# Gate and up products in two matmuls instead of three, with halves that are added behind, and a first column group in one piece

## The chip, the cores and the metric

The program runs on one core of a Trainium2 chip. The metric is device time in microseconds, from launch to end. The kernel before was timed three times: 1051.45, 1048.04 and 1046.29, median 1048.04. One further execution was profiled, and the profile's lines come from that one.

## The reference

A decoder trunk of two layers over 256 rows of 1024 columns, in float32. Each layer is a SwiGLU block, a token mixer (gated DeltaNet in layer 0, sliding-window attention in layer 1) and a second SwiGLU block, each behind an RMSNorm; a last RMSNorm follows. Cut to what matters here:

```python
D_FF = 2816                                   # ((8 * 1024 // 3 + 127) // 128) * 128

def swiglu(h, w_gu, w_down):                  # h: (1, 256, 1024), w_gu: (1024, 2 * 2816), w_down: (2816, 1024)
    gate, up = jnp.split(h @ w_gu, 2, axis=-1)
    return (jax.nn.silu(gate) * up) @ w_down

for layer in range(2):
    x = x + 0.5 * swiglu(rmsnorm(x, ffn1_norm[layer]), ffn1_w_gu[layer], ffn1_w_down[layer])
    x = x + mixer(rmsnorm(x, mix_norm[layer]))
    x = x + 0.5 * swiglu(rmsnorm(x, ffn2_norm[layer]), ffn2_w_gu[layer], ffn2_w_down[layer])
return rmsnorm(x, final_norm)
```

So four SwiGLU blocks run, with a gate and up product of 1024 by 5632 weights each.

## The kernel before

**Precision.** TensorE works on one-pass operands (type float32r). Each float32 operand is therefore split exactly into a high and a low part, and one product is made of three: high by high, high by low and low by high (`mm3`, lines 307 to 311). The rows' operand after a norm is `hh` and `hl`, transposed, 128 partitions by 8 tiles of the 1024 columns by 256 rows. Weights come from memory in pieces of 512 KB into `raw`, are cast to the high part `whi` by ScalarE (ACT, line 275), and VectorE (DVE) subtracts that from `raw` to get `wlo` (line 276). `raw` has 4 buffers, `whi` and `wlo` 5 each, so a piece can be cast only when the matmuls have let go of the one five before it. The loads are issued by SyncE (SP) in the order of use.

**Gate and up.** `ffn` (line 329) walks over 11 groups `c` of 256 gate columns and 256 up columns. A group's weights are two pieces for gate and two for up (`wcols`). In groups 1 to 10 the weight is the stationary operand and the 256 rows stream past it: `proj_T` makes, for each of 2 column tiles `f` and 8 tiles `k` of the inner dimension, the three matmuls of `mm3`, 256 columns wide, all into the same half bank of PSUM (`pg` or `pu`, from a pool of 4 banks). ScalarE takes Silu of `pg` into `sg` (line 338), VectorE multiplies it with `pu` into `act` (line 340), GpSimd (POOL) rounds that to `ah` (line 389) and VectorE subtracts to get `al` (line 390): the two parts of the operand for the down product. The matmuls of one `k`, `f` and of gate or up are called a **unit** below: three matmuls, three weight loads. There are 4 blocks x 10 groups x 2 x 2 x 8 = 1280 units.

Group 0 is done the other way round (`part_N`): the rows are stationary, 128 at a time (`t` is 0 or 1), the weight streams, 256 columns of gate into `pg` and 256 of up into `pu`; the result `act` is turned by two transposes (`pat`, line 378). This lets rows 0 to 127 start while rows 128 to 255 are still in the norm: the transposes `psT` (line 89) of those rows stand between the two halves of group 0.

**The first block** starts before its norm is known: it multiplies x times the norm's weight (`hh0`, `hl0`) and scales behind; GpSimd then scales the operand `f` itself in four pieces (line 183), and from those come `hh`, `hl` for groups 1 to 10 (lines 185, 186). The second half of x is loaded by `late()`, called between gate's and up's weights of group 0.

**Down** streams the weight rows, 512 columns wide, past `ah` and `al`, in units of three matmuls too (`acc`); in the last block some of them are 256 wide. The mixers use `proj_T` and `proj_N` with their three matmuls.

Instructions of an engine run in the order that a list scheduler gave them from its own estimate of times when the program was built; an engine does not overtake within its order.

Of the kernel before, what the change touches and what calls it, by code (L numbers as in the profile page):

```python
# [15 lines left out]
P = 128  # L16
D = 1024
T = 256
# [36 lines left out]

class Norm:
    """RMSNorm of the residual into a transposed, exactly split operand hh + hl."""

    def __init__(self, kern, wrow):
        self.k = kern  # L60
        self.w = kern.n4([P, D], "nw")
        kern.nc.scalar.dma_start(out=self.w, in_=wrow.partition_broadcast(P))
        self.hh = self.hl = None
# [17 lines left out]
    def tile(self, t):  # L81
        k, nc = self.k, self.k.nc
        if self.hh is None:
            self.hh = k.big([P, KT, T], "hh", F32R)
            self.hl = k.big([P, KT, T], "hl", F32R)
        for q, (xn, s) in enumerate(self.rows(t)):
# [11 lines left out]
    def piece(self, t, s, sq):  # L98
        """Of a row's piece, x * w and the sum of the squares."""
# [25 lines left out]
class First(Norm):  # L125
    """The first norm: the rows' factor comes late, so the first products take x * w and are scaled behind."""

    def __init__(self, kern, wrow):
# [4 lines left out]
        self.hh0, self.hl0 = k.big([P, KT, T], "hh0", F32R), k.big([P, KT, T], "hl0", F32R)  # L133
        self.hh, self.hl = k.big([P, KT, T], "hh", F32R), k.big([P, KT, T], "hl", F32R)
# [3 lines left out]
    def raw(self, t):  # L138
# [7 lines left out]
        for q in range(2):  # L146
# [7 lines left out]
            oh = self.hh0[:, ks, ts]  # L154
            nc.scalar.copy(oh, f)
            nc.vector.tensor_sub(self.hl0[:, ks, ts], f, oh.bitcast(F32))
# [14 lines left out]
    def scale(self):  # L171
# [8 lines left out]
        for q in range(4):  # L180
# [3 lines left out]
            oh = self.hh[:, ks]  # L184
            nc.scalar.copy(oh, f)
            nc.vector.tensor_sub(self.hl[:, ks], f, oh.bitcast(F32))  # L186


class Kern:
# [60 lines left out]
    def warm(self, n):  # L250
        """Products that nobody reads, while the first loads are under way: the array's clock rises with its use."""
# [10 lines left out]
    def split(self, src, hi, lo, shape, eng=None):  # L262
# [49 lines left out]

    def proj_T(self, out, w, f, nrm):
        fs = slice(f * P, (f + 1) * P)
        for k in range(KT):
            wh, wl = w(k, fs)
            self.mm3(out, wh, wl, nrm.hh[:, k, :], nrm.hl[:, k, :], k == 0, k == KT - 1)

    def proj_N(self, out, w, t, nrm):
        self.part_N(out, w, t, nrm.hh, nrm.hl, range(KT))  # L320

    def part_N(self, out, w, t, hh, hl, ks):
        ts = slice(t * P, (t + 1) * P)
        for k in ks:
            wh, wl = w(k, slice(0, 256))
            self.mm3(out, hh[:, k, ts], hl[:, k, ts], wh, wl, k == 0, k == KT - 1)

# [1 line left out]
    def ffn(self, nrm, w_gu, w_down, after, mid=None, late=None, final=None):  # L329
# [6 lines left out]
        def glu(pg, pu):  # L336
            sg = self.c1([P, T], "sg")
            ahead[0] = nc.scalar.activation(sg, pg[:, :T], AF.Silu)
            a = self.c1([P, T], "act")
            ahead[1] = nc.vector.tensor_mul(a, sg, pu[:, :T])  # L340
            return a

        for c in range(DFF // 256):
# [5 lines left out]
            wg = self.wcols(w_gu, c * 256)  # L349
            if c == 0 and late is not None:  # L350
                late()
            wu = self.wcols(w_gu, DFF + c * 256)
            pgs = [None] * 2
            if c == 0 and late is not None:
                pgs = [(self.psA("pg"), self.psA("pu")) for t in range(NT)]
                for n, w in ((0, wg), (1, wu)):
                    for ks in (range(0, 4), range(4, 8)):
# [921 lines left out]
```

## Time and profile before

| | us |
|---|---|
| median of three runs | 1048.04 (1046.29 to 1051.45) |
| profiled execution: span from first to last instruction | 1048.2 |
| PE (TensorE's matmuls) busy in it | 1021.5 |
| DVE busy | 625.9 |
| ACT busy | 498.8 |
| POOL busy | 220.4 |

The profiled execution's own time is its span: nothing outside the first and last instruction is recorded, and the span lies 0.2 us from the median. Its stages, by the starts of PE's rows: gate and up of the first block from 11 to 144 us, down to 205, DeltaNet to 387, second block to 576, third to 766, attention to 852, fourth block to 1042.

How to read the lines: a matmul's row gives its start, its length and the width of what streams (`128x256` is 256 columns). Matmuls are pipelined, so rows overlap; what one costs in a dense stream is the distance from its start to the next start, not its length. PEld is the weight load, which has a row of its own. In groups of instructions the columns are line, engine, operation, out<-in, shapes, count, then busy us and mean ns of one, then the idle time of the engine just before and what ended it.

### The profile page before, as it was taken

How to read it: one execution, taken by the hardware profiler on the slowest of the kernel's cores; microseconds unless marked ns; L12 is line 12 of the kernel's file. 1: busy time of each engine (PE TensorE's matmuls, PEld its weight loads, DVE VectorE, ACT ScalarE, POOL GpSimd, SP SyncE). 2: the span in 40 equal slices, each digit the busy share in tenths (PEclk: the TensorE clock that was granted, in tenths of full speed). 3: DMA queues.
4: the chain of work that ended last, by engine and by line, in shares of the span. 5: the costliest groups of instructions: out<-in, count | busy, mean ns of one | idle time of the engine just before them, and what ended most of it. 6: DMA issues, size and time to landing. Idle time of an engine off the chain costs nothing.

```text
span 1048.2 us, 18944 instructions
## 1 busy us (share of the span) xinstructions
PE 1021.5 (97%) x7683; PEld 956.2 (91%) x7683; DVE 625.9 (60%) x887; ACT 498.8 (48%) x847; POOL 220.4 (21%) x197
## 2 busy tenths in 40 slices
PE   8999999999979999999999999999999999999997
PEld 7999998899979889999988999998899689999986
DVE  5755554666895665565545655554568856555544
ACT  5544443557755544443434433444456644344432
POOL 3123410006743201122100022120021401221100
PEclk9999999999989999999999999999999999999999
DMA  7666666654442335566565566567653426655661
GB/s 225 188 192 186 183 213 190 186 156 130 133 141 83 120 101 162 161 187 200 195 195 179 173 190 190 163 195 217 215 180 123 133 89 191 201 172 173 212 196 43
DMA packets 135003, 177.20 MB, mean 169 GB/s; under 512 B 6930, under 2 KB 119940, under 8 KB 134916
## 3 DMA queue, kind: packets, MB, share of 16 engines
q1 hardware_dynamic: 131712, 171.46, 52.6%
q10 hardware_dynamic: 3204, 4.53, 1.4%
q8 instruction: 60, 0.98, 0.4%
q14 instruction: 27, 0.22, 0.1%
HBM read 174.92 MB, written 1.05 MB: 168 GB/s over the span
## 4 chain that ended last, share of the span: by engine, by line
PE 62%; issue 1%; DVE 1%; ACT 0%; POOLq 0%; POOL 0%; ACTq 0%
PE acc L311 7%; PE acc L309 7%; PE acc L310 7%; PE pg L309 6%; PE pg L311 6%; PE pu L311 6%; PE pu L309 6%; PE pu L310 6%; PE pg L310 6%; PE pq L309 1%; PE pq L311 1%; PE pq L310 1%; PE psc L1103 1%; PE po L1147 1%; PE psT L89 1%
## 5 line engine op out<-in xcount | busy, mean ns | idle before, releaser
L275 ACT CAST whi<-raw 128x1024 fp32r<-128x1024 f32 x316 | 330.0, 1051 | 313.9 <-PE pg L310 161.5
L276 DVE TENSOR_TENSOR wlo<-raw,whi 128x1024 fp32r<-128x1024 f32 x302 | 382.1, 1268 | 154.3 <-ACT whi L275 153.8
L389 POOL TENSOR_SCALAR ah<-act 128x256 fp32r<-128x256 f32 x80 | 103.5, 1294 | 389.9 <-DVE act L340 389.9
L310 PE MATMUL pg<-hl,whi 128*128 128x256 f32 x640 | 181.2, 283 | 1.0 <-DVE hl L186 1.0
L310 PE MATMUL pu<-hl,whi 128*128 128x256 f32 x640 | 181.3, 283 | 0.0
L311 PE MATMUL pg<-hh,wlo 128*128 128x256 f32 x640 | 181.2, 283 | 0.0
L309 PE MATMUL pu<-hh,whi 128*128 128x256 f32 x640 | 181.2, 283 | 0.0
L311 PE MATMUL pu<-hh,wlo 128*128 128x256 f32 x640 | 181.2, 283 | 0.0
L309 PE MATMUL pg<-hh,whi 128*128 128x256 f32 x640 | 181.1, 283 | 0.0
L310 PE MATMUL acc<-wlo,ah 128*128 128x512 f32 (+1 forms) x340 | 128.4, 378 | 0.0
L311 PE MATMUL acc<-whi,al 128*128 128x512 f32 (+1 forms) x340 | 128.2, 377 | 0.0
L309 PE MATMUL acc<-whi,ah 128*128 128x512 f32 (+1 forms) x340 | 127.9, 378 | 0.0
L310 PEld LDWEIGHTS pg<-hl,whi 128*128 128x128 f32 x640 | 122.9, 192 | 1.2 <-DVE hl L186 1.2
L311 PEld LDWEIGHTS pg<-hh,wlo 128*128 128x128 f32 x640 | 122.9, 192 | 0.0
L309 PEld LDWEIGHTS pg<-hh,whi 128*128 128x128 f32 x640 | 122.9, 192 | 0.0
L311 PEld LDWEIGHTS pu<-hh,wlo 128*128 128x128 f32 x640 | 122.8, 192 | 0.0
L309 PEld LDWEIGHTS pu<-hh,whi 128*128 128x128 f32 x640 | 122.8, 192 | 0.0
L310 PEld LDWEIGHTS pu<-hl,whi 128*128 128x128 f32 x640 | 122.8, 192 | 0.0
L340 DVE TENSOR_TENSOR act<-sg,pu 128x256 f32<-128x256 f32 x86 | 35.9, 418 | 98.0 <-PE pu L311 96.2
L309 PEld LDWEIGHTS acc<-whi,ah 128*128 128x128 f32 x340 | 64.0, 188 | 11.9
L311 PEld LDWEIGHTS acc<-whi,al 128*128 128x128 f32 x340 | 63.9, 188 | 12.0
L310 PEld LDWEIGHTS acc<-wlo,ah 128*128 128x128 f32 x340 | 64.0, 188 | 11.7
(343 smaller groups left out, 1623.5 us busy)
## 6 DMA issues: line engine op xcount, KB each, us to landing
raw<-in_ffn_w_gu_dram SPq DMA_DIRECT2D x176, 512.0 KB, 4.9
raw<-in_ffn_w_down_dram SPq DMA_DIRECT2D x88, 512.0 KB, 4.3
raw<-in_a_w_in_dram SPq DMA_DIRECT2D x32, 512.0 KB, 4.5
raw<-in_b_w_in_dram SPq DMA_DIRECT2D x12, 512.0 KB, 4.9
raw<-in_a_w_out_dram SPq DMA_DIRECT2D x8, 512.0 KB, 3.9
raw<-in_b_w_out_dram SPq DMA_DIRECT2D x8, 512.0 KB, 3.8
nw<-in_ffn_norm_dram ACTq DMA_DIRECT2D x3, 512.0 KB, 4.1
x<-in_x_dram SPq DMA_DIRECT2D x2, 512.0 KB, 7.1
```

Of the source, the lines that this page charges most:

```text
L89: last = nc.tensor.transpose(ps[:, i * P:(i + 1) * P], xn[:, s.start + i * P:s.start + (i + 1) * P], k.ident)
L275: nc.scalar.copy(hi, raw)
L276: (eng or nc.vector).tensor_tensor(out=lo, in0=raw, in1=hi.bitcast(F32), op=ALU.subtract)
L309: nc.tensor.matmul(out, lhsT=lh, rhs=rh, start=start, stop=False)
L310: nc.tensor.matmul(out, lhsT=lh, rhs=rl, start=False, stop=False)
L311: return nc.tensor.matmul(out, lhsT=ll, rhs=rh, start=False, stop=stop)
L340: ahead[1] = nc.vector.tensor_mul(a, sg, pu[:, :T])
L389: ahead[2] = nc.gpsimd.tensor_scalar(oh, a, 1.0, None, op0=ALU.mult)
L1103: nc.tensor.matmul(out, lhsT=qT[:, j, b * P:(b + 1) * P], rhs=kz[:, kv, :, kt * P:(kt + 1) * P], start=True, stop=True)
L1147: lastpo[0] = nc.tensor.matmul(po[64 * i:64 * i + 64, b * P:(b + 1) * P], lhsT=v[:, kt, kv * HD:(kv + 1) * HD], rhs=pT[:, b + kt, i, :], s ...
```

## The change

Three things change.

1. The two parts of the rows' operand lie side by side: class `Split` holds two tiles of 128 x 4 x 2 x 256, so that high part and low part of one `k` are 512 neighbouring columns (`both`). A unit of groups 1 to 10 becomes two matmuls (`mm2`, `proj_T2`): the weight's high part against all 512 columns, into a whole PSUM bank, and the weight's low part against the high rows, 256 columns, added to the bank's first half.
2. The two halves of the bank are added behind: ScalarE copies the second half to SBUF (`gate` or `act`), VectorE adds the first half. Silu is then taken in place, and the product of gate and up moves from VectorE to GpSimd. Gate's two column tiles now come before up's two.
3. Group 0 loads gate and up columns together (`wpairs`): four pieces of 2 tiles `k` by 512 columns, each loaded by two DMAs. Its three matmuls of `part_N` are 512 wide and fill one bank `pgu`. `late()` is called behind all four pieces instead of behind the first two. Silu and the product behind it both wait for the same bank.

The mixers keep `mm3`, with the parts taken from `Split`.

```diff
+class Split:
+    def __init__(self, kern):
+        self.parts = [kern.big([P, 4, 2, T], "hs", F32R) for _ in range(2)]
+    def four(self, q, ts):
+        return tuple(self.parts[q][:, :, e, ts] for e in range(2))
+    def both(self, k):
+        return self.parts[k // 4][:, k % 4].rearrange("p e t -> p (e t)")
+    def hi(self, k, ts=slice(0, T)):
+        return self.parts[k // 4][:, k % 4, 0, ts]
+    def lo(self, k, ts=slice(0, T)):
+        return self.parts[k // 4][:, k % 4, 1, ts]
...
-            oh = self.hh[:, 4 * q:4 * q + 4, t * P:(t + 1) * P]
+            oh, ol = self.h.four(q, slice(t * P, (t + 1) * P))
             hi = nc.scalar.copy(oh, pv)
-            lo = nc.vector.tensor_sub(self.hl[:, 4 * q:4 * q + 4, t * P:(t + 1) * P], pv, oh.bitcast(F32))
+            lo = nc.vector.tensor_sub(ol, pv, oh.bitcast(F32))
...
-        nc.sync.dma_start(out=raw, in_=src)
+        if inner is None:
+            nc.sync.dma_start(out=raw, in_=src)
+        else:
+            for k in range(shape[1]):
+                nc.sync.dma_start(out=raw[:, k].rearrange("p (g f) -> p g f", g=2), in_=src[:, k])
...
+    def wpairs(self, w, c0):
+        src = w.rearrange("(k p) (g f) -> p k g f", p=P, g=2)[:, :, :, c0:c0 + 256]
+        pieces = []
+        for i in range(4):
+            hi = self.wp.tile([P, 2, 512], F32R, tag="whi", name="whi")
+            lo = self.wp.tile([P, 2, 512], F32R, tag="wlo", name="wlo")
+            self.split(src[:, 2 * i:2 * i + 2], hi, lo, [P, 2, 512], inner="p k (g f) -> p k g f")
+            pieces.append((hi, lo))
+        return lambda k, cs: tuple(a[:, k % 2, cs] for a in pieces[k // 2])
...
+    def mm2(self, out, lh, ll, r2, rh, start, stop):
+        nc = self.nc
+        nc.tensor.matmul(out, lhsT=lh, rhs=r2, start=start, stop=False)
+        return nc.tensor.matmul(out[:, :T], lhsT=ll, rhs=rh, start=False, stop=stop)
+    def proj_T2(self, out, w, f, h):
+        fs = slice(f * P, (f + 1) * P)
+        for k in range(KT):
+            wh, wl = w(k, fs)
+            mm = self.mm2(out, wh, wl, h.both(k), h.hi(k), k == 0, k == KT - 1)
+        return mm
...
+            if c == 0:
+                w = self.wpairs(w_gu, 0)
+                ps = [self.psA("pgu") for t in range(NT)]
+                if late is not None:
+                    late()
+                    for ks in (range(0, 2), range(2, 4), range(4, 6), range(6, 8)):
                         for t in range(NT):
-                            self.part_N(pgs[t][n][:, :T], w, t, nrm.hh0, nrm.hl0, ks)
+                            self.part_N(ps[t], w, t, nrm.h0, ks)
...
+                    if late is None:
+                        nc.scalar.activation(sg, ps[t][:, :T], AF.Silu)
+                        nc.vector.tensor_mul(a, sg, ps[t][:, T:])
...
-                    self.proj_T(pg[:, :T], wg, f, nrm)
-                    self.proj_T(pu[:, :T], wu, f, nrm)
-                    a = glu(pg, pu)
-                    ff = 2 * c + f
-                    oh = ah[ff // 8][:, ff % 8, :]
-                    ahead[2] = nc.gpsimd.tensor_scalar(oh, a, 1.0, None, op0=ALU.mult)
-                    nc.vector.tensor_sub(al[ff // 8][:, ff % 8, :], a, oh.bitcast(F32))
+            gates = []
+            wg = self.wcols(w_gu, c * 256)
+            for f in range(2):
+                pg = self.psA("pg")
+                self.proj_T2(pg, wg, f, nrm.h)
+                g = self.c1([P, T], "gate")
+                nc.scalar.copy(g, pg[:, T:])
+                nc.vector.tensor_tensor(out=g, in0=g, in1=pg[:, :T], op=ALU.add)
+                ahead[0] = nc.scalar.activation(g, g, AF.Silu)
+                gates.append(g)
+            wu = self.wcols(w_gu, DFF + c * 256)
+            for f in range(2):
+                pu = self.psA("pu")
+                self.proj_T2(pu, wu, f, nrm.h)
+                a = self.c1([P, T], "act")
+                nc.scalar.copy(a, pu[:, T:])
+                ahead[1] = nc.vector.tensor_tensor(out=a, in0=a, in1=pu[:, :T], op=ALU.add)
+                nc.gpsimd.tensor_tensor(out=a, in0=a, in1=gates[f], op=ALU.mult)
+                ff = 2 * c + f
+                oh = ah[ff // 8][:, ff % 8, :]
+                ahead[2] = nc.gpsimd.tensor_scalar(oh, a, 1.0, None, op0=ALU.mult)
+                nc.vector.tensor_sub(al[ff // 8][:, ff % 8, :], a, oh.bitcast(F32))
```

Where the instructions stand now is shown at three places. Names are the program's tiles, with the number of the buffer's use; `xN` is a row that stands N times.

**PE, group 0 of the second block, at the seam between rows 0 to 127 and rows 128 to 255.** Before, the last up products of the first rows, then the transposes of the second rows, then those of `act`, then gate and up of the second rows in turn, with their high rows first:

```order
L310 MATMUL pu_4494<-wlo_4488,hh_4359 128x256
L311 MATMUL pu_4494<-whi_4487,hl_4360 128x256
L89 MATMUL psT_4446<-ident_70,xn_4438 128x128 x4
L89 MATMUL psT_4454<-ident_70,xn_4438 128x128 x4
L378 MATMUL pat_4547<-ident_70,act_4545 128x128 x2
L309 MATMUL pg_4552<-whi_4469,hh_4359 128x256
L310 MATMUL pg_4552<-wlo_4470,hh_4359 128x256
L309 MATMUL pu_4553<-whi_4481,hh_4359 128x256
```

After, at the same place:

```order
L342 MATMUL pgu_4211<-wlo_4205,hs_4074 128x512
L343 MATMUL pgu_4211<-whi_4204,hs_4074 128x512
L107 MATMUL psT_4160<-ident_70,xn_4152 128x128 x4
L107 MATMUL psT_4168<-ident_70,xn_4152 128x128 x4
L412 MATMUL pat_4241<-ident_70,act_4238 128x128 x2
L341 MATMUL pgu_4212<-whi_4183,hs_4073 128x512
L342 MATMUL pgu_4212<-wlo_4184,hs_4073 128x512
L343 MATMUL pgu_4212<-whi_4183,hs_4073 128x512
```

The transposes `pat` stand at the same distance from the last product as before, but that product now ends gate as well as up, so Silu is no longer done ahead of it.

**ACT in a middle group of the first block.** Before, between two casts of weights stands one Silu:

```order
L338 ACTIVATE sg_540<-pg_490 128x256
L275 CAST whi_608<-raw_610 128x1024
L275 CAST whi_614<-raw_616 128x1024
L338 ACTIVATE sg_596<-pg_546 128x256
L275 CAST whi_620<-raw_622 128x1024
```

After:

```order
L424 COPY gate_446<-pg_429 128x256
L433 COPY act_479<-pu_462 128x256
L426 ACTIVATE gate_446<-gate_446 128x256
L296 CAST whi_568<-raw_570 128x1024
L296 CAST whi_620<-raw_622 128x1024
L433 COPY act_502<-pu_485 128x256
```

Two copies, one of gate and one of up, and a Silu now stand between two pairs of casts; the Silu waits for VectorE's add.

**SP at the start.** Before, the second load of x stands behind two pieces of weights:

```order
L1211 DMA x_81<-in_x_dram 128x1024
L265 DMA raw_136<-in_ffn1_w_gu_dram 128x4x256
L265 DMA raw_142<-in_ffn1_w_gu_dram 128x4x256
L1211 DMA x_81<-in_x_dram 128x1024
L265 DMA raw_165<-in_ffn1_w_gu_dram 128x4x256
L265 DMA raw_171<-in_ffn1_w_gu_dram 128x4x256
```

After, behind four, each loaded by two DMAs:

```order
L1260 DMA x_81<-in_x_dram 128x1024
L286 DMA raw_136<-in_ffn1_w_gu_dram 128x2x256 x2
L286 DMA raw_143<-in_ffn1_w_gu_dram 128x2x256 x2
L286 DMA raw_150<-in_ffn1_w_gu_dram 128x2x256 x2
L286 DMA raw_157<-in_ffn1_w_gu_dram 128x2x256 x2
L1260 DMA x_81<-in_x_dram 128x1024
```

The second half of x moved behind two more pieces, 1 MB. From the down products through the mixers the order of PE's instructions is what it was.

More of the change, by code (lines that the diff above doesn't have):

```diff
@@ L82, in tile @@
         k, nc = self.k, self.k.nc
[L83 to L85 removed]
+        if self.h is None:
+            self.h = Split(k)
         for q, (xn, s) in enumerate(self.rows(t)):
@@ L153, in raw @@
                                     in1=self.wT[:, ks].unsqueeze(2).to_broadcast([P, 4, P]), op=ALU.mult)
-            oh = self.hh0[:, ks, ts]
+            oh, ol = self.h0.four(q, ts)
             nc.scalar.copy(oh, f)
-            nc.vector.tensor_sub(self.hl0[:, ks, ts], f, oh.bitcast(F32))
+            nc.vector.tensor_sub(ol, f, oh.bitcast(F32))
         return tr
@@ L183, in scale @@
             nc.gpsimd.tensor_tensor(out=f, in0=f, in1=rb.unsqueeze(1).to_broadcast([P, 2, T]), op=ALU.mult)
-            oh = self.hh[:, ks]
+            oh, ol = (self.h.parts[q // 2][:, 2 * (q % 2):2 * (q % 2) + 2, e] for e in range(2))
             nc.scalar.copy(oh, f)
-            nc.vector.tensor_sub(self.hl[:, ks], f, oh.bitcast(F32))
+            nc.vector.tensor_sub(ol, f, oh.bitcast(F32))
 class Kern:
@@ L334, in ffn @@
         ahead = [None] * 3
[L336 to L341, printed above, removed]
         for c in range(DFF // 256):
@@ L348, in ffn @@
                     mid()
[L349 to L357, printed above, removed]
+            if c == 0:
[4 more added lines that the diff above has]
+                    for ks in (range(0, 2), range(2, 4), range(4, 6), range(6, 8)):
@@ L358, in ffn @@
                         for t in range(NT):
-                            self.part_N(pgs[t][n][:, :T], w, t, nrm.hh0, nrm.hl0, ks)
+                            self.part_N(ps[t], w, t, nrm.h0, ks)
+                    for t in range(NT):
+                        nrm.factor(t)
+                    nrm.scale()
                 for t in range(NT):
-                    nrm.factor(t)
-                nrm.scale()
-            for f in range(2):
-                pg, pu = pgs[f] or (self.psA("pg"), self.psA("pu"))
-                if c == 0:
-                    if pgs[f] is None:
-                        self.proj_N(pg[:, :T], wg, f, nrm)
-                        self.proj_N(pu[:, :T], wu, f, nrm)
-                        a = glu(pg, pu)
-                    else:
-                        sg = self.c1([P, T], "sg")
-                        nc.scalar.activation(sg, pg[:, :T], AF.Silu, scale=nrm.r[f])
-                        a = self.c1([P, T], "act")
-                        nc.vector.scalar_tensor_tensor(out=a, in0=pu[:, :T], scalar=nrm.r[f], in1=sg,
+                    if late is None:
+                        self.proj_N(ps[t], w, t, nrm)
@@ L375, in ffn @@
+                    sg = self.c1([P, T], "sg")
+                    a = self.c1([P, T], "act")
+                    if late is None:
+                        nc.scalar.activation(sg, ps[t][:, :T], AF.Silu)
+                        nc.vector.tensor_mul(a, sg, ps[t][:, T:])
+                    else:
+                        nc.scalar.activation(sg, ps[t][:, :T], AF.Silu, scale=nrm.r[t])
+                        nc.vector.scalar_tensor_tensor(out=a, in0=ps[t][:, T:], scalar=nrm.r[t], in1=sg,
                                                        op0=ALU.mult, op1=ALU.mult)
```

27 lines of the change are left out of this document (13 added, 14 removed).

## The prediction

> **What bounds the kernel now.** I read the page first: busy time, clock, chain.
>
> ```profile
> span 1048.2 us, 18944 instructions
> PE 1021.5 (97%) x7683; PEld 956.2 (91%) x7683; DVE 625.9 (60%) x887; ACT 498.8 (48%) x847; POOL 220.4 (21%) x197
> ...
> PEclk9999999999989999999999999999999999999999
> ...
> PE 62%; issue 1%; DVE 1%; ACT 0%; POOLq 0%; POOL 0%; ACTq 0%
> ```
>
> PE is busy 97% of the span at nearly full clock, and the chain of waits that ended last is PE's own. A busy PE may still wait for data, so next comes the view of stretches, of gate and up in the second block (columns: stretch, its us, then busy us and count of PE, PEld, DVE, ACT, POOL, clock, DMA share, GB/s), and after it the timeline of PE in the first block.
>
> ```profile
> 400.00:510.00 110.00, 110.00 (x919) 110.00 (x919) 60.97 (x78) 45.91 (x58) 23.50 (x18) 1.00 0.61 191
> ```
>
> ```profile
> 59.92 0.28 PE L309 MATMUL pg<-hh,whi 128*128 128x256 f32 x1
> ...
> 63.88 0.28 PE L309 MATMUL pg<-hh,whi 128*128 128x256 f32 x1
> ```
>
> 919 matmuls in 110.00 us are 119.7 ns each; 33 steps between the two rows, 3.96 us, are 120.0 ns. No pause lies between. The next rows are down products, 512 columns wide, 9 steps in 2.04 us:
>
> ```profile
> 159.83 0.39 PE L309 MATMUL acc<-whi,ah 128*128 128x512 f32 x1
> ...
> 161.87 0.39 PE L309 MATMUL acc<-whi,ah 128*128 128x512 f32 x1
> ```
>
> That is 226.7 ns. Doubling the columns adds 106.7 ns, so 256 columns cost 106.7 ns of streaming and a matmul has **13.3 ns fixed beside it**, at both widths. One form in the trace has a weight half as wide, `pab`, 128*64, 256 columns streaming:
>
> ```profile
> 215.88 0.28 PE L309 MATMUL pab<-hh,wabh 128*64 128x256 f32 x1
> ...
> 216.90 0.28 PE L309 MATMUL pab<-hh,wabh 128*64 128x256 f32 x1
> ```
>
> 9 steps in 1.02 us: 113.3 ns, 6.7 fixed. The fixed part halves with the weight's columns, so it belongs to the weight load, and whoever saves a load saves it.
>
> **The change part by part.** *Groups 1 to 10.* A unit takes 3 x 120 = 360 ns. After, it is one matmul of 512 and one of 256 columns: 226.7 + 120 = 346.7 ns. The columns streamed are the same 768; one weight load goes. 1280 units x 13.3 ns = **17.1 us**, all on PE's dense stream, which sets the end.
>
> This takes each width's price from a stream of its own width. Widths alternate in the trace only in the last block's down product:
>
> ```profile
> 990.87 0.39 PE L311 MATMUL acc<-whi,al 128*128 128x512 f32 x1
> 991.10 0.28 PE L309 MATMUL acc<-whi,ah 128*128 128x256 f32 x1
> 991.21 0.28 PE L310 MATMUL acc<-wlo,ah 128*128 128x256 f32 x1
> 991.33 0.28 PE L311 MATMUL acc<-whi,al 128*128 128x256 f32 x1
> ...
> 991.81 0.40 PE L309 MATMUL acc<-whi,ah 128*128 128x512 f32 x1
> 992.05 0.40 PE L310 MATMUL acc<-wlo,ah 128*128 128x512 f32 x1
> 992.28 0.39 PE L311 MATMUL acc<-whi,al 128*128 128x512 f32 x1
> ...
> 993.88 0.28 PE L309 MATMUL acc<-whi,ah 128*128 128x256 f32 x1
> ```
>
> Behind a wide matmul the first narrow one takes 110 (991.10 to 991.21), behind narrow ones the first wide one 240 and the second 230 (rows are rounded to 10 ns). The whole cycle of 9 wide and 6 narrow, 991.10 to 993.88, takes 2.78 us, where 9 x 226.7 + 6 x 120 = 2.76: one change of width there and back costs about 20 ns. In the new stream the width changes with every matmul. Ends of the range: wide at its steady 226.7 with narrow at 110, a pair of 337, saves 23.3 ns a unit, 29.8 us; the full 20 ns paid in each pair, 366.7, loses 6.7 ns a unit, 8.5 us. The rows at a single change of width, 240 and 110, add up to 350, about the additive 346.7, and what came on top (the second wide one) stands where the new stream has a narrow one. I take 346.7.
>
> *Group 0.* Two halves x 24 matmuls of 512 for 96 of 256: 48 x (240 - 226.7) ns = 0.64 us a block, **2.6 us** in four. Here one width follows itself.
>
> *The seam in group 0* of the last three blocks, PE's rows with the engines it waits for:
>
> ```profile
> 392.67 0.28 PE L311 MATMUL pu<-whi,hl 128*128 128x256 f32 x1
> 392.80 1.04 PE L89 MATMUL psT<-ident,xn 128*128 128x128 f32 x8
> 393.67 0.38 PE L378 MATMUL pat<-ident,act 128*128 128x128 f32 x2
> 394.07 0.39 PE L309 MATMUL pg<-whi,hh 128*128 128x256 f32 x1
> ```
>
> ```profile
> 390.36 0.39 ACT L338 ACTIVATE sg<-pg 128x256 f32<-128x256 f32 x1 [1.67 <-PE pg L311]
> ```
>
> ```profile
> 393.07 0.42 DVE L340 TENSOR_TENSOR act<-sg,pu 128x256 f32<-128x256 f32 x1 [2.05 <-PE pu L311]
> ```
>
> Silu stood 2.7 us ahead of the product; now both wait for the same matmul. From that matmul's start X: it ends at X + 0.39, Silu 0.39, product 0.42, and 0.12 to 0.18 to hand over each time (as 392.95 to 393.07 and 393.49 to 393.67): `pat` at X + 1.6 and the second rows' first product at X + 1.8, against 394.07 - 392.67 = 1.4. The transposes cover only 0.9 of it. **0.35 us lost** a block, about 1 us in three. In the first block other products stand there.
>
> *The start.* The second half of x now lands behind 1 MB more. The rows of ACT, POOL, DVE and PE, and the stretch that has the DMA rate:
>
> ```profile
> 11.00:16.50 5.50, 4.33 (x23) 3.93 (x23) 4.10 (x7) 3.65 (x7) 0.55 (x1) 0.69 1.07 343
> ```
>
> ```profile
> 12.80 0.63 ACT L164 ACTIVATE xn<-x 128x512 f32<-128x512 f32 x1
> ```
>
> ```profile
> 19.46 7.79 POOL L183 TENSOR_TENSOR f<-f,rb 128x512 f32<-128x512 f32 x4 [4.13 <-DVE hl L156]
> ```
>
> ```profile
> 19.84 4.56 DVE L276 TENSOR_TENSOR wlo<-raw,whi 128x1024 fp32r<-128x1024 f32 x2
> ```
>
> ```profile
> 29.00 0.39 PE L310 MATMUL pg<-hl,whi 128*128 128x256 f32 x1 [0.96 <-DVE hl L186]
> ```
>
> 1.05 MB at 343 GB/s are 3.1 us, by which ACT's squares, GpSimd's scaling and the 0.96 us wait behind it can come later. Against that, PE does the first rows' wide products meanwhile: while the clock is low (0.69) 12 matmuls carry 512 columns where they carried 256, some 1.4 us of the later stream, and groups 0 and 1 have 1.1 us less to do (0.64 + 0.43). I put it at **1 us lost**, between 1.5 gained and 4 lost.
>
> *What is added behind.* Each column tile (8 units) gets a copy from PSUM on ACT and an add on DVE; the product goes to POOL. Prices:
>
> ```profile
> L275 ACT CAST whi<-raw 128x1024 fp32r<-128x1024 f32 x316 | 330.0, 1051 | 313.9 <-PE pg L310 161.5
> L276 DVE TENSOR_TENSOR wlo<-raw,whi 128x1024 fp32r<-128x1024 f32 x302 | 382.1, 1268 | 154.3 <-ACT whi L275 153.8
> L389 POOL TENSOR_SCALAR ah<-act 128x256 fp32r<-128x256 f32 x80 | 103.5, 1294 | 389.9 <-DVE act L340 389.9
> ```
>
> ```profile
> L810 POOL TENSOR_TENSOR wq<-wq,qT 128x256 f32<-128x256 f32 x4 | 3.7, 926 | 16.3 <-ACT qT L838 16.3
> ```
>
> A group takes PE 32 x 346.7 = 11.1 us. ACT in it: 4 casts x 1.05, 4 copies and 2 Silus at about the Silu's 0.39: 6.5 us. DVE: 4 x 1.27, 4 adds and 2 subtractions x 0.42: 7.6. POOL: 2 x (1.29 + 0.93): 4.4. All stay below 11.1. ACT now waits in its order for two banks before it casts again, but casts wait for PE anyway (161.5 us, for a free buffer), and gate's weights are let go earlier, when gate's two columns are done. PSUM has 4 banks and a column fills one in 2.8 us, so a bank may come back 8 us late. I cost it at nothing; without that cover each microsecond of delay in all 40 groups would be 40 us.
>
> That POOL's product has two inputs in SBUF matters for DVE: under POOL's scaling the two `wlo` (4.56 us) take 2.28 each, not 1.27. Two products a group at worst double 1.9 us of DVE: 9.5 of 11.1. The Trainium skill (GPSIMD Engine Reference, Key points) says that GpSimd shares its SBUF interfaces with VectorE and contends with VectorE instructions of two SBUF inputs, which would speak against moving the product there; the trace agrees on the contention, and if DVE were the bound it would cost up to 1.9 us x 40 = 76 us, but it is not.
>
> Sum on the profiled execution: 1048.2 - 17.1 - 2.6 + 1 + 1 = **1030.5 us**. The span lies 0.2 us from the median of the runs, so the same stands for a median.
>
> **The rivals.** *Changes of width cost*, the one that ends slower. Place: every second matmul of groups 1 to 10; price: up to 20 ns a unit, as in the last block's cycle. It decides from (17.1 + 2.6 - 2) / 1280 = 13.8 ns a unit on. At 20 ns: 1048.2 + 8.5 - 2.6 + 2 = 1056. Against it: the 20 ns come at the second and later wide matmuls. *Part of it*: the wide one at the 240 of the change and the narrow one at its steady 120, 360 a unit, save nothing there; half of that, 353, saves 8.5: 1039. *Narrow matmuls hide their load* behind wide ones, pair 337: 1048.2 - 29.8 - 2.6 + 2 = 1018. *Evacuation holds PE* at the ends of columns, ACT's order being the likely place: 0.25 us a group x 40 = 10 us, 1040; the cover above speaks against it. *It doesn't do what it says*: the load that goes was hidden, the 13.3 ns belong to the columns, the wide matmul takes 240: group 0 saves nothing either, 1048.2 + 2 = 1050; the down rows at 226.7 speak against it.
>
> The Trainium skill (TensorE: Matmul & The Clock Gate, Back-to-back issue gap) gives an isolated matmul N / 2.4 + 2.5 ns: a unit would go from 328 to 325 ns and 1280 units would save an estimated 3 us. No row here has a surplus as small as 2.5; by 13.3 measured at two widths the sum stands.
>
> **How the numbers follow.** Forecast 0.62, part of it 0.12, evacuation 0.08, full price of the changes 0.07, hidden loads 0.06, not what it says 0.05. The forecast's own range is 1027 to 1036: the start's bounds and a unit that is 2 ns dearer or cheaper. To leave out no more than 2 in 10, the range reaches to the partial case and the evacuation above, and takes half of the hidden-load case below: **1023 to 1042**. Half a per cent, 5.2 us, is about what a measurement of this kernel can tell from no change. Below 1042.8 lie the forecast, the hidden loads and most of the partial and evacuation cases: faster 0.84. Within it: their tails and half of the last case, 0.07. Slower: the full price and the rest, 0.09.
>
> **What would show it.** In the timeline of a middle group: starts of wide and narrow 347 ns a pair, no pause; 353 or more is the price of changing width, 337 the hidden load. PE's groups of `pg` and `pu` four instead of six, 640 each, and as many fewer weight loads. Gate and up of a block from its first to its last product shorter by 4.9 us less 0.35. `pat` 1.6 us behind the last product of the first rows. At the start, the wait for the low part in group 1 near 29 us, and the end of group 1 within 3 us of the old. PE rows with an idle time ended by ACT or DVE inside groups 2 to 10 would make the forecast wrong, as would a DVE busy all through a group.

## The result, and the profile after

The changed kernel took 1029.92 us (median of four runs, 1029.09 to 1030.38), the kernel before beside it 1048.53 (1046.29 to 1051.45): a ratio of **0.9822, 95% interval 0.9805 to 0.9839**. Both were run again later: 1032.67 against 1049.13, ratio 0.9838 (0.9814 to 0.9861). The forecast was 1030.5, in a range of 1023 to 1042.

First the page of the changed kernel, the lines that answer to those shown of before.

```profile
span 1028.6 us, 16500 instructions
...
PE 1003.0 (98%) x6211; PEld 873.3 (85%) x6211; DVE 649.5 (63%) x967; ACT 552.5 (54%) x1007; POOL 244.8 (24%) x277
...
PEclk9999999999989999999999999999999999999999
...
PE 62%; issue 1%; DVE 1%; ACT 1%; POOLq 0%; POOL 0%; ACTq 0%
```

7683 matmuls have become 6211: 1280 fewer in groups 1 to 10, 192 fewer in group 0. PE's busy time fell by 18.5 us, its weight loads' by 82.9. PE is the bound as before, now at 98%. The other engines have more to do (DVE 649.5 for 625.9, ACT 552.5 for 498.8, POOL 244.8 for 220.4) and none of it shows in the chain.

Next, from the same page, the groups of the new instructions (line, engine, operation, out<-in, shapes, count, then busy us and mean ns, then idle time before them and what ended it).

```profile
L297 DVE TENSOR_TENSOR wlo<-raw,whi 128x1024 fp32r<-128x1024 f32 x302 | 379.9, 1260 | 202.7 <-ACT whi L296 201.7
...
L348 PE MATMUL pg<-hs,whi 128*128 128x512 f32 x640 | 225.6, 394 | 0.3 <-DVE hs L203 0.3
L348 PE MATMUL pu<-hs,whi 128*128 128x512 f32 x640 | 225.1, 393 | 0.0
L349 PE MATMUL pu<-hs,wlo 128*128 128x256 f32 x640 | 179.7, 281 | 0.3 <-DVE wlo L297 0.3
L349 PE MATMUL pg<-hs,wlo 128*128 128x256 f32 x640 | 178.9, 280 | 0.0
...
L435 POOL TENSOR_TENSOR act<-act,gate 128x256 f32<-128x256 f32 x80 | 60.2, 752 | 346.5 <-DVE act L434 337.7
...
L438 POOL TENSOR_SCALAR ah<-act 128x256 fp32r<-128x256 f32 x80 | 69.0, 862 | 6.8
...
L424 ACT COPY gate<-pg 128x256 f32<-128x256 f32 x80 | 29.5, 369 | 58.9 <-PE pg L349 58.9
```

The wide matmul is `L348`, the narrow one `L349`. Up's 1280 waited 0.3 us in all, for a weight, and gate's 1280 0.3 us, for the rows' low part in group 1 of the first block: no bank came back late. The copies cost 369 ns where 390 was taken, the product on POOL 752 where 926 was, and `wlo` is no dearer (1260 ns, before 1268).

The view of stretches, the same 110 us of the second block as before (stretch, its us, busy us and count of PE, PEld, DVE, ACT, POOL, clock, DMA share, GB/s):

```profile
400.00:510.00 110.00, 110.00 (x628) 96.65 (x627) 69.93 (x100) 60.60 (x97) 31.82 (x40) 1.00 0.65 193
```

PE is busy throughout, and VectorE has 40 us to spare. How a unit runs shows in PE's timeline, first in the second block:

```profile
400.09 0.39 PE L348 MATMUL pu<-hs,whi 128*128 128x512 f32 x1
400.32 0.28 PE L349 MATMUL pu<-hs,wlo 128*128 128x256 f32 x1
400.43 0.39 PE L348 MATMUL pu<-hs,whi 128*128 128x512 f32 x1
...
401.13 0.39 PE L348 MATMUL pu<-hs,whi 128*128 128x512 f32 x1
```

Three units from 400.09 to 401.13, 1.04 us: 346.7 ns each, the forecast's price. In the first block the same instructions run like this:

```profile
60.15 0.28 PE L349 MATMUL pu<-hs,wlo 128*128 128x256 f32 x1
60.27 0.40 PE L348 MATMUL pu<-hs,whi 128*128 128x512 f32 x1
60.51 0.28 PE L349 MATMUL pu<-hs,wlo 128*128 128x256 f32 x1
60.62 0.40 PE L348 MATMUL pg<-hs,whi 128*128 128x512 f32 x1
60.85 0.28 PE L349 MATMUL pg<-hs,wlo 128*128 128x256 f32 x1
...
61.21 0.28 PE L349 MATMUL pg<-hs,wlo 128*128 128x256 f32 x1
```

Three units from 60.15 to 61.21, 1.06 us: **353.3 ns each**, in steps of 120 and 236, 113 and 233, 117 and 241 ns, over and over. I call the first an even rhythm and this one a three-beat rhythm. It was not foreseen.

Stages by the starts of PE's rows, in us, with a second profile of each kernel from the experiments below:

| | before | before, again | after | after, again |
|---|---|---|---|---|
| group 2 of the first block begins at | 40.48 | 38.87 | 38.01 | 41.26 |
| groups 2 to 10 of the first block | 103.56 | 103.56 | 101.64 | 101.64 |
| DeltaNet, to the second block's first product | 181.78 | 181.46 | 179.06 | 179.44 |
| second block's gate and up, first to last product | 128.30 | 128.29 | 123.71 | 123.73 |
| third block's | 128.30 | 128.30 | 123.77 | 123.79 |
| attention | 86.03 | 86.03 | 87.21 | 87.23 |
| fourth block's | 128.31 | 128.29 | 123.73 | 123.73 |

The rows of blocks 2 to 4 repeat to 0.03 us and carry 13.7 us of the 19.6 between the first and the third column's spans. The first row does not repeat at all, and DeltaNet and attention, which the change leaves as they were, differ too. Those three needed explaining besides the gain itself.

### The profile page after: what moved, and what is told of

Its sections match the earlier page's. It is cut to its first block, busy times and chain, and to the rows that moved or that the text cites. A ratio compares the mean times of both kernels' runs of the same rounds, so it can differ in the third digit from the quotient of the medians.

```text
span 1028.6 us, 16500 instructions
## 1 busy us (share of the span) xinstructions
PE 1003.0 (98%) x6211; PEld 873.3 (85%) x6211; DVE 649.5 (63%) x967; ACT 552.5 (54%) x1007; POOL 244.8 (24%) x277
## 4 chain that ended last, share of the span: by engine, by line
PE 62%; issue 1%; DVE 1%; ACT 1%; POOLq 0%; POOL 0%; ACTq 0%
PE pg L348 11%; PE pu L348 11%; PE acc L343 7%; PE acc L341 7%; PE acc L342 7%; PE pu L349 6%; PE pg L349 6%; PE pgu L343 1%; PE pgu L342 1%; PE pgu L341 1%; PE pq L341 1%; PE pq L343 1%; PE pq L342 1%; PE psc L1152 1%; PE po L1196 1%
## 5 line engine op out<-in xcount | busy, mean ns | idle before, releaser
L297 DVE TENSOR_TENSOR wlo<-raw,whi 128x1024 fp32r<-128x1024 f32 x302 | 379.9, 1260 | 202.7 <-ACT whi L296 201.7
L348 PE MATMUL pg<-hs,whi 128*128 128x512 f32 x640 | 225.6, 394 | 0.3 <-DVE hs L203 0.3
L348 PE MATMUL pu<-hs,whi 128*128 128x512 f32 x640 | 225.1, 393 | 0.0
L349 PE MATMUL pu<-hs,wlo 128*128 128x256 f32 x640 | 179.7, 281 | 0.3 <-DVE wlo L297 0.3
L349 PE MATMUL pg<-hs,wlo 128*128 128x256 f32 x640 | 178.9, 280 | 0.0
L348 PEld LDWEIGHTS pg<-hs,whi 128*128 128x128 f32 x640 | 119.9, 187 | 27.7 <-DVE hs L203 0.7
L348 PEld LDWEIGHTS pu<-hs,whi 128*128 128x128 f32 x640 | 119.8, 187 | 27.0
L435 POOL TENSOR_TENSOR act<-act,gate 128x256 f32<-128x256 f32 x80 | 60.2, 752 | 346.5 <-DVE act L434 337.7
L349 PEld LDWEIGHTS pu<-hs,wlo 128*128 128x128 f32 x640 | 120.9, 189 | 0.6 <-DVE wlo L297 0.6
L349 PEld LDWEIGHTS pg<-hs,wlo 128*128 128x128 f32 x640 | 120.9, 189 | 0.4
L341 PE MATMUL pcv<-hs,whi 128*128 128x256 f32 x192 | 56.5, 294 | 5.9 <-DVE cv L883 5.9
```

The costliest lines, as they stand in the source:

```text
L297: (eng or nc.vector).tensor_tensor(out=lo, in0=raw, in1=hi.bitcast(F32), op=ALU.subtract)
L341: nc.tensor.matmul(out, lhsT=lh, rhs=rh, start=start, stop=False)
L348: nc.tensor.matmul(out, lhsT=lh, rhs=r2, start=start, stop=False)
L349: return nc.tensor.matmul(out[:, :T], lhsT=ll, rhs=rh, start=False, stop=stop)
L435: nc.gpsimd.tensor_tensor(out=a, in0=a, in1=gates[f], op=ALU.mult)
```

## The experiments

The theory, A: the gain is the saved weight load, 13.3 ns each, on PE's dense stream. Rivals: B, it comes from group 0 and the start; C, from the layout, the order or the evacuation, the load having been hidden. Ratios are to the kernel before, run beside each.

### 1 and 2: each half of the change alone

Experiment 1 has group 0 as before, experiment 2 has groups 1 to 10 as before, both on the operand that lies side by side.

```diff
 # 1: group 0
-                w = self.wpairs(w_gu, 0)
-                ps = [self.psA("pgu") for t in range(NT)]
+                wg = self.wcols(w_gu, 0)
                 if late is not None:
                     late()
...
+                wu = self.wcols(w_gu, DFF)
...
 # 2: groups 1 to 10
-                self.proj_T2(pg, wg, f, nrm.h)
...
+                self.proj_T(pg[:, :T], wg, f, nrm)
+                self.proj_T(pu[:, :T], wu, f, nrm)
...
```

> Only groups 1 to 10 changed; group 0 has its four pieces, its 96 matmuls of 256 columns and the second rows' load behind two pieces, as before. Theory A (the saved weight load of each unit makes the gain): most of it stays, the changed kernel's 1029.9 plus 2.6 (group 0's loads), less 1 (the seam), plus what the start gained, some 1.4: about 1033. Theory B (the gain comes from group 0 and the start): back to 1045 or more. On the first block's 353.3 ns a unit: if it hangs on where the rows' operand lies, it stays, since the operand lies in the same place; if it hangs on how the stream is entered, it may turn to 346.7.

> Only group 0 changed; groups 1 to 10 make their three matmuls of 256 columns with Silu and the product as before, on the operand that lies side by side. Theory A: 1048.5 less 2.6 for group 0's loads, plus 1 for the seam, less 0 to 1.4 at the start: 1045.5 to 1047, and a unit takes 360 ns in all four blocks. Theory B: near 1033.

Measured: experiment 1 **1032.48**, ratio 0.9861 (0.9839 to 0.9883). Experiment 2 **1045.39**, ratio 0.9979 (0.9967 to 0.9990). Groups 2 to 10 of blocks 2 to 4 take 99.72 us in experiment 1, as in the changed kernel, and 103.56 in experiment 2, as before; from the first start to the last these are 287 units and the first steps of the last one (0.23 and 0.24 us), so 346.7 and 360.0 ns a unit. The whole of gate and up in those blocks: 124.24 to 124.26 in experiment 1 (4.05 to 4.06 less than before), 127.75 to 127.81 in experiment 2 (0.49 to 0.55 less), and together that is the changed kernel's 4.5 to 4.6. The halves add up; B falls. In experiment 1 the first block's groups 2 to 10 took 99.72 too, with the operand in the same place: the 353.3 does not hang on that place.

### 3: everything as changed, but the load not saved

```diff
-        nc.tensor.matmul(out, lhsT=lh, rhs=r2, start=start, stop=False)
+        nc.tensor.matmul(out[:, :T], lhsT=lh, rhs=r2[:, :T], start=start, stop=False)
+        nc.tensor.matmul(out[:, T:], lhsT=lh, rhs=r2[:, T:], start=False, stop=False)
```

> The changed kernel with its layout, banks, evacuation, order and group 0, but the wide matmul of groups 1 to 10 cut into two of 256 columns, each with its own load of the same high part. Theory A: a unit takes 360 ns again, 1029.9 plus 13.3 ns x 960 units of blocks 2 to 4 plus 6.7 ns x 320 of the first: plus 14.9, about 1044.8. Theory C (layout, order or evacuation make the gain, and the load was hidden): stays within 2 us of 1029.9.

Measured: **1044.47**, ratio 0.9972 (0.9959 to 0.9986). PE's timeline of this kernel in the second block:

```profile
449.97 0.28 PE L348 MATMUL pu<-hs,whi 128*128 128x256 f32 x1
...
450.93 0.28 PE L350 MATMUL pu<-hs,wlo 128*128 128x256 f32 x1
```

Eight steps in 0.96 us, 120 ns each, and 360 a unit. Layout, banks, copies, adds and order are the changed kernel's; only the second load of the same weights is back, with a matmul of its own, and 14.5 us with it by the medians (13.6 by the gate and up stages of the two profiles). C falls. Every matmul here has its load, so this run can't tell the two apart; that the price is the load's rests on the prediction's rows of a weight half as wide, which cost 6.7 ns where a whole one costs 13.3.

The Trainium skill (TensorE: Matmul & The Clock Gate, Back-to-back issue gap) gives a matmul of N columns N / 2.4 + 2.5 ns when it stands alone. By that, 1280 more matmuls with the same columns would cost an estimated 3.2 us here; the run says 14.5, and the measurement decides.

### 4: the second rows' load behind two pieces

```diff
         for i in range(4):
+            if i == 2 and late is not None:
+                late()
             hi = self.wp.tile([P, 2, 512], F32R, tag="whi", name="whi")
...
-                    late()
```

> The changed kernel with the second rows of x loaded behind two of the four first pieces, not behind all four. The start term of the prediction (1.05 MB ahead of those rows delay the scaling and what waits behind it, plus 1 us, up to plus 4): the rows land some 3 us earlier and group 2 begins 1 us or more before 38.0 us. Rival (the second rows cost nothing there, since the first rows' wide products fill the time while the clock is low): group 2 begins no earlier, or up to 3 us later, since two pieces of weights now land later and the products of the first rows wait for them; total between 1029.9 and 1033.

Measured: 1030.27, ratio 0.9825 (0.9808 to 0.9841), no different from the changed kernel. Group 2 began at 37.84, not the 1 us earlier that was expected. It did so although this execution's clock from 11 to 18 us was 0.76 (7 us x 0.24 = 1.7 us lost), while the changed kernel's was 1.00. That led to the clock at the start, below; as a time the run decides nothing.

### 5: wide matmuls first

```diff
         for k in range(KT):
-            wh, wl = w(k, fs)
-            mm = self.mm2(out, wh, wl, h.both(k), h.hi(k), k == 0, k == KT - 1)
+            nc.tensor.matmul(out, lhsT=w(k, fs)[0], rhs=h.both(k), start=k == 0, stop=False)
+        for k in range(KT):
+            mm = nc.tensor.matmul(out[:, :T], lhsT=w(k, fs)[1], rhs=h.hi(k), start=False, stop=k == KT - 1)
```

> Each column tile of groups 1 to 10 makes its 8 wide matmuls first and its 8 narrow ones behind, so the width changes twice a column and not sixteen times. If widths add up (226.7 and 120 each) and the first block's 353.3 comes of alternating: blocks 2 to 4 unchanged, the first block 2.1 us shorter, about 1027.8. If each change there and back costs the 20 ns of the last block's down product: 160 columns x 20 ns = 3.2 more, about 1031 with the first block's 2.1 won. If alternating in blocks 2 to 4 hides something, a column there takes longer than 8 x 346.7 ns = 2.77 us.

Measured: **1032.86**, ratio 0.9860 (0.9844 to 0.9875). PE's timeline of this kernel joins equal rows here; a column of 8 units runs from wide to wide:

```profile
450.12 2.00 PE L355 MATMUL pg<-hs,whi 128*128 128x512 f32 x8
451.96 1.12 PE L357 MATMUL pg<-hs,wlo 128*128 128x256 f32 x8
452.91 2.00 PE L355 MATMUL pg<-hs,whi 128*128 128x512 f32 x8
```

2.79 us a column, where 8 x 346.7 is 2.77. Groups 2 to 10 take 100.44 us in every block, 0.72 more than alternating: 20 ns for each of 36 columns. The total was expected at about 1031 and came 1.9 above it; the profiled execution lost 1.7 us to a low clock at its start. So the 20 ns of a single change of width, which the prediction read in the last block, is real, and it is *not* paid in the even rhythm, where the width changes with every matmul. (In the three-beat one, three units take 1.06 us for 1.04: 20 ns once in three units.) The rival "changes of width cost" had the right price and the wrong place.

### 6, 7 and 9: where the first block's rhythm comes from

Two transposes that nobody reads are put into PE's stream, either between a wide matmul and its narrow one ("in") or ahead of the next wide one ("between").

```diff
+            if k == 4 and cut == "in":
+                wide = self.nc.tensor.matmul(out, lhsT=wh, rhs=h.both(k), start=False, stop=False)
+                with self.tc.issue_after(wide.ins):
+                    turn = self.two_turns()
+                with self.tc.issue_after(turn.ins):
+                    mm = self.nc.tensor.matmul(out[:, :T], lhsT=wl, rhs=h.hi(k), start=False, stop=False)
+                continue
```

> Two transposes nobody reads are put into PE's stream of group 2: in the first block between a wide matmul and its narrow one, in the third block between a narrow one and the next wide one. If the 353.3 ns a unit of the first block is a rhythm that goes on until something breaks it, and where the break falls decides the next rhythm: the first block falls to 346.7 from there on, the third rises to 353.3 from there on, the second and fourth stay. If it belongs to the first block's data, its place or its loads: nothing changes but 0.3 us each for the transposes.

> Only the first block's two transposes. If the rhythm theory holds: groups 2 to 10 of the first block 101.64 us less some 1.8, plus 0.3 for the transposes, and the whole at about 1028.4, 1.5 below the changed kernel. Otherwise 1030.2.

> In blocks 2, 3 and 4, which run at 346.7 ns a unit, two pairs of transposes nobody reads are put into group 2: the first between a narrow matmul and the next wide one, the second 6, 7 and 8 units later between a wide matmul and its narrow one (blocks 2, 3 and 4 in this order). Theory of rhythms: the first turns the stream to 353.3, as in the third block of the run before; the second turns it back in block 2, where it falls at the same point of the slow rhythm as the transposes of act do in every later block (behind a wide matmul that started 120 ns behind a narrow one); groups 2 to 10 then take 99.7 plus 0.6 us there. In blocks 3 and 4 the point is another one: 100.3 too if any break turns it back, 102.1 if only that point does. Rival (inserted work itself makes a stream slow): 102.1 in all three.

Measured: 1034.22 (6, one run), 1031.09 with ratio 0.9839 (0.9825 to 0.9854) (7), 1033.39 (9, one run). Experiment 6's third block, from PE's timeline, `turn` being the two transposes:

```profile
591.47 0.28 PE L350 MATMUL pg<-hs,wlo 128*128 128x256 f32 x1
...
591.82 0.28 PE L350 MATMUL pg<-hs,wlo 128*128 128x256 f32 x1
591.94 0.38 PE L375 MATMUL turn<-ident 128*128 128x128 f32 x2
592.07 0.48 PE L349 MATMUL pg<-hs,whi 128*128 128x512 f32 x1
...
592.86 0.40 PE L349 MATMUL pg<-hs,whi 128*128 128x512 f32 x1
593.10 0.28 PE L350 MATMUL pg<-hs,wlo 128*128 128x256 f32 x1
593.22 0.40 PE L349 MATMUL pg<-hs,whi 128*128 128x512 f32 x1
593.46 0.28 PE L350 MATMUL pg<-hs,wlo 128*128 128x256 f32 x1
```

Ahead of the break the narrow matmuls stand 0.35 us apart, the even rhythm; from 592.86 on it is 0.24, 0.12, 0.24, the three-beat one, and it goes on to the block's end: groups 2 to 10 took 101.83 us for 99.72. That block is otherwise untouched, so **neither rhythm belongs to data, place or loads.** In the changed kernel such breaks are there anyway: the transposes of `act` (`pat`) fall into group 1. In the second, third and fourth block the stream runs in three beats up to them and evenly for the 298 units behind; in the first block it ran evenly up to them and in three beats for the 297 behind. In the second profile of the same kernel the first block ran in three beats on both sides, and in the profiles of experiments 1 and 10 its groups 2 to 10 took 99.72 us, the even rhythm.

Which way a break turns it stays open. In experiment 7 the break in the first block met an even stream and made it three-beat (281 units behind it), so the hoped-for gain was a loss. In experiment 6 a three-beat first block stayed as it was. In experiment 9 the first break turned only the third block, and there the second turned it back; groups 2 to 10 took 100.18 to 100.22 us in all three blocks. That matches a number of the expectation, but not the reason given for it, since the stream of blocks 2 and 4 was never turned. What holds in all of them: away from such breaks and from waits the rhythm does not change.

### 8: the product back on VectorE

```diff
-                nc.gpsimd.tensor_tensor(out=a, in0=a, in1=gates[f], op=ALU.mult)
+                nc.vector.tensor_tensor(out=a, in0=a, in1=gates[f], op=ALU.mult)
```

> The changed kernel with the product of gate and up back on VectorE. The prediction's term (the added work on ACT, DVE and POOL is hidden): 80 x 0.42 us more on DVE, 80 x 0.75 less on POOL, and the time stays at 1029.9 within 1 us. Rival (the move to GpSimd carries part of the gain, DVE being near its limit): some us slower, with waits of PE for weights in groups 2 to 10.

Measured: 1030.62, ratio 0.9839 (0.9821 to 0.9857), span 1028.6 as in the changed kernel. The same stretch of the second block in this kernel:

```profile
400.00:510.00 110.00, 110.00 (x628) 96.65 (x627) 78.59 (x120) 60.43 (x97) 17.05 (x20) 1.00 0.61 193
```

DVE has 8.7 us more, POOL 14.8 less, PE's row is the same to its last digit: where the product stands costs nothing either way. The contention that the prediction priced hardly arose: in the changed kernel's profile only 2 of the 80 products on GpSimd ran beside a `wlo` on VectorE (in one case the `wlo` took 1.62 us for a usual 1.22, in the other the product 1.69 for 0.74), so what many such meetings would cost is not tested here.

### 10 to 12: the clock at the start, and both kernels again

```diff
 # 10, on top of experiment 4
-        K.warm(8)
+        K.warm(20)
...
+                            if t == 0 and ks.start == 0:
+                                with self.tc.issue_after(mm.ins):
+                                    nrm.raw(1)
```

> The second rows' load behind two pieces, as in the run before, and 20 instead of 8 products nobody reads ahead of the first real one; the second rows' transposes are held behind the first 6 products. Theory (the start's clock is cut where PE idles 2 us or more ahead of the first product, and that costs 1.1 to 1.3 us): the clock stays at 1.00 from 11 to 17 us, group 2 begins at 36.5 to 37 us, against 38.0 in the changed kernel at full clock and 39.1 to 39.4 at the low one; total about 1 us below the changed kernel. Rival (the low clock there does not come from that idle): clock near 0.5 for 13 to 15 us and group 2 at 37.8 or later.

> The changed kernel once more, unchanged, to stand beside the run before on the same chip: 1029.9 within 1 us. If the start's clock and the first block's rhythm are matters of the single execution, its profile may show group 2 at 39.1 to 39.4 with a low clock, or groups 2 to 10 of the first block at 99.7; if they belong to the program, it shows 38.0 and 101.6 again.

> The kernel before once more, unchanged, for a second profile of it. Theory (the 2.7 us that DeltaNet came out shorter in the changed kernel's profile, the 1.2 us that attention came out longer, and the start's spread are the granted clock of single executions): DeltaNet differs from the first profile's 181.8 us by 1 us or more, attention takes 86.0 or 87.2, group 2 begins up to 2.5 us from 40.5; gate and up of blocks 2 to 4 take 128.3 us each again, to 0.1. Rival (the changed kernel makes DeltaNet shorter, through what it leaves loaded or through the place of the operand): 181.8 again within 0.3, and attention 86.0.

Measured: experiment 10 1030.74 (1028.34 to 1033.68), ratio 0.9810 (0.9786 to 0.9835); the changed kernel beside it 1032.67, ratio 0.9838 (0.9814 to 0.9861); the kernel before again 1047.97 (one run). The two ratios' intervals overlap, so experiment 10 is not shown to be faster. The stretch from 11 to 18 us, its third last number the clock, in the first profile of before:

```profile
11.00:18.00 7.00, 5.83 (x35) 5.43 (x36) 5.60 (x10) 4.82 (x10) 0.55 (x1) 0.76 0.92 295
```

in its second profile:

```profile
11.00:18.00 7.00, 5.84 (x46) 5.53 (x47) 6.87 (x12) 6.08 (x12) 0.71 (x2) 1.00 0.90 288
```

in the changed kernel's first:

```profile
11.00:18.00 7.00, 6.49 (x32) 5.20 (x33) 6.12 (x9) 5.72 (x9) 0.55 (x1) 1.00 1.09 360
```

and in its second:

```profile
11.00:18.00 7.00, 6.24 (x15) 4.66 (x16) 5.58 (x6) 5.87 (x9) 0.56 (x1) 0.52 1.01 330
```

Time lost is 7 us times what the clock lacks of 1: 1.7, 0, 0 and 3.4 us, and group 2 began at 40.48, 38.87, 38.01 and 41.26. The differences within each kernel, 1.6 and 3.2, are the lost time, to 0.2 us. **One program, two executions, 3.2 us apart at the start.** At full clock before and after are 0.9 us apart. Experiment 10 had 1.00 and began group 2 at 37.16, 0.2 above what was expected; but with 8 such products experiment 9 had 1.00 as well, so it is not shown that the longer run of them did it. The fourteen profiles bear the theory out in part: in seven of the eight with a low clock at the start PE had idled 2.0 to 3.5 us ahead of its first product, and in five of the six at full clock less than 2. The exceptions are the first profile of before (1.15 us and low) and experiment 9 (2.21 and full); that the idle time is the cause is not shown. The changed kernel beside experiment 10 was expected at 1029.9 within 1 us and came 2.8 above that. Group 2 began 3.2 us later in its profile than in the first one, while the first block's groups 2 to 10 took 101.64 again.

DeltaNet the same way, the whole stage: before, before again, the changed kernel, again, experiments 9 and 10.

```profile
205.27:387.04 181.77, 169.06 (x1643) 159.12 (x1642) 131.46 (x255) 109.02 (x278) 69.06 (x52) 0.97 0.41 121
```

```profile
203.65:385.11 181.46, 169.12 (x1643) 159.16 (x1642) 132.00 (x255) 108.95 (x278) 68.04 (x52) 0.97 0.40 121
```

```profile
200.85:379.92 179.07, 167.35 (x1644) 157.37 (x1643) 131.43 (x255) 109.05 (x278) 69.09 (x52) 0.98 0.41 123
```

```profile
204.09:383.54 179.45, 167.71 (x1644) 157.71 (x1643) 131.45 (x255) 109.20 (x278) 69.08 (x52) 0.98 0.40 123
```

```profile
201.31:382.70 181.39, 169.77 (x1643) 159.73 (x1642) 131.56 (x255) 109.22 (x278) 69.07 (x52) 0.97 0.39 121
```

```profile
198.12:383.26 185.14, 173.01 (x1643) 162.59 (x1642) 131.83 (x255) 109.12 (x278) 67.40 (x52) 0.94 0.39 119
```

The stage's length follows its clock, to about 1 us. In stretches of 2 us the lost time is 5.1, 5.1, 3.4, 3.4, 5.1 and 10.3 us, and the low clock is 0.50 each time. So the clock makes 1.7 of the 2.7 us between the two first profiles. The length less the lost time lies between 174.9 and 176.7 us in all fourteen profiles, with before at 176.3 and 176.7, the changed kernel at 175.7 and 176.0 and its variants 1 and 4 at 176.6, so the other 1.0 is no more than variants that leave this stage alone differ by. Experiment 9 runs the changed kernel's instructions up to the end of DeltaNet and took 181.4 there, so the changed kernel can take as long as before. Still the expectation that before would differ from itself by 1 us was missed: 181.8 and 181.5. Whether the change makes the third low stretch rarer stays open: 5.1 us or more were lost in both profiles of before, in experiment 2 and in two of the eleven others. Attention's 86.0 or 87.2 is one low stretch more (the changed kernel's clock was 0.79 from 814 to 822 us, that of before 1.00 from 830 to 838). Of the fourteen profiles, eight at full clock there took 86.0 to 86.1 us and six with one low stretch 87.1 to 87.3; among the six is experiment 2, with the groups of before, and among the eight are experiments 4 and 7, with those of the changed kernel.

The lost times are multiples of 1.7 us, which at half clock is 3.4 us of low clock. The Trainium skill (TensorE: Matmul & The Clock Gate, Part 1: The HAM clock gate) says that the clock is set in free-running windows of about 3.4 us, to half or full, so that the same kernel's low stretches vary from run to run; the traces agree on the length, the two levels and the variation, and that the windows run free of the kernel is not shown here.

## Why the prediction was right, and where not

| step | predicted | measured |
|---|---|---|
| groups 1 to 10, blocks 2 to 4 | -12.8 | -12.2 (experiment 1) |
| groups 2 to 10, first block | -3.8 | -1.9 |
| group 0 with its seam, blocks 2 to 4 | -0.9 | -1.6 (experiment 2) |
| first block up to group 2 | -0.1 | -2.5; at full clock -0.9 |
| DeltaNet and attention | 0 | -2.7 and +1.2 |
| span | -17.7 | -19.6 |

**The price of a load** held: in groups 2 to 10 of the later blocks 3.84 us for 288 loads, 13.3 ns each, and experiment 3 gave it back. That 12.2 came and not 12.8 is 0.21 us a block. Of that, 0.07 are the 11 units of group 1 that still run in three beats up to `pat`, and some 0.13 stand at the seam of experiment 1, where a wait that a matmul of group 1 filled before is now empty.

**Additive widths** held there and failed in the first block. The forecast had "2 ns dearer or cheaper" as the unit's own range; the three-beat rhythm is 6.7 dearer, the price that the rival "part of it" put on all blocks. It holds one block, from a break on; why that break turned the stream there is open.

**The seam** was taken at 0.35 us and cost 0.02 to 0.08 up to the second rows' first product: 1.52 to 1.58 us from the last product of the first rows to the first of the second, for 1.40, and 0.107 of the difference is the wider product itself, which has its price elsewhere. The timeline of the changed kernel:

```profile
385.13 0.40 PE L343 MATMUL pgu<-whi,hs 128*128 128x512 f32 x1
...
385.56 0.38 ACT L404 ACTIVATE sg<-pgu 128x256 f32<-128x256 f32 x1 [4.00 <-PE pgu L343]
385.98 0.42 DVE L405 TENSOR_TENSOR act<-sg,pgu 128x256 f32<-128x256 f32 x1 [2.08 <-ACT sg L404]
...
386.46 0.44 PE L412 MATMUL pat<-ident,act 128*128 128x128 f32 x2
...
386.65 0.49 PE L341 MATMUL pgu<-whi,hs 128*128 128x512 f32 x1
...
386.97 0.40 PE L342 MATMUL pgu<-wlo,hs 128*128 128x512 f32 x1
...
387.36 0.50 PE L343 MATMUL pgu<-whi,hs 128*128 128x512 f32 x1
...
387.70 0.40 PE L341 MATMUL pgu<-whi,hs 128*128 128x512 f32 x1
```

Hand-overs from engine to engine take 0.03 to 0.06 us here (385.53 to 385.56, 385.94 to 385.98, 386.40 to 386.46), not the 0.12 to 0.18 that I took; `pat` comes 1.33 us behind that product's start, not 1.6. The whole seam cost more, 0.09 to 0.15 us a block (0.64 from the loads, less the 0.49 to 0.55 of experiment 2): the second rows' first products follow each other in 0.32, 0.39 and 0.34 us, where the steady step is 0.23.

**The start** was put at 1 us lost. At full clock in both, group 2 began 0.4 to 0.9 us earlier (38.01, 38.05 and 38.47 in the changed kernel and experiments 8 and 9, for 38.87), of which the loads explain 1.07: 0.2 to 0.7 lost. The sign was right and the size a little high. The -2.5 of the two first profiles is mostly clock.

**The added work** cost nothing, as taken; the rival "evacuation holds PE" falls with the 0.3 us above, and "narrow matmuls hide their load" with the pairs, none of which came at 337 ns. (The working's four banks of PSUM are the pool that the program gives these products.)

**Span and time.** The working set the profiled span equal to the median. An execution's time is in fact 1.7 us above its own span (1030.34 with a span of 1028.6), so its 1030.5 was a sum of spans. By that the profiled execution of before took about 1049.9 us, an estimate, which is above the median: the two errors nearly cancel. The span fell to 1028.6. That 1029.92 lies so near the forecast is partly chance: the first block and DeltaNet missed on opposite sides, and in the later runs of both kernels the gain was 16.5 us, not 18.6.

## What to carry to other kernels

Where PE streams without a pause, count weight loads, not only columns: the fixed part per matmul can be read from starts at two widths, and an operand that meets the same weights twice can be laid side by side and meet them once. Before crediting a change with a stage that it leaves alone, profile both kernels twice and look at the clock of that stage; here 3 us at the start and 2 in DeltaNet came and went between executions of the same instructions, most of it with the clock. A price read at one change of state, such as 20 ns a change of width, need not hold for a stream that changes at every step.

## What was not expected of the hardware

The same stream of alternating 512 and 256 columns has two stable rhythms, 346.7 and 353.3 ns a pair. In these traces it keeps one for some 300 pairs and changes it only at a break, even one of two transposes; where widths change only twice in 16 matmuls, a change there and back costs 20 ns.
